# Neighbourhood attention layer on one core: less filler in the first steps, rows split directly, a block of x loaded again earlier

## The chip, the cores and the metric

The kernel runs on one core of one Trainium2 chip. The metric is device time in microseconds (us): 1064.29 us as the median of three runs (1062.66 to 1065.86). The engines are named as in the profile: PE is TensorE (matrix products), PEld its weight loads, DVE is VectorE, ACT is ScalarE, POOL is GpSimd, SP issues nearly all DMAs.

## The reference

One layer of neighbourhood attention over a grid of 32 rows by 64 columns (2048 tokens, 1024 features, 16 heads of 64), in float32:

```python
h = rmsnorm(x, norm_0)
q, k, v, gate = split(h @ w_in, 4)
for each grid row r:                       # rs: first of 8 key rows
    s = q . k * scale                      # 16 query columns against 8 x 32 keys
    s = where(column in window, s + bias, -1e30)
    o = softmax(s) @ v
x = x + (o * silu(gate)) @ w_out
return rmsnorm(x, norm_f)
```

## The kernel before

**Precision.** Every large product is done as three products of float32r parts: an operand is split into h (a copy on ACT) and l = t - h (a subtraction on DVE), and h*h, h*l, l*h are summed in PSUM. So each operand block of 128 x 512 that TensorE uses costs one ACT and one DVE instruction (`split_to`, L441 to L447; the lines of the profile are 443 and 444).

**Stages.** `stage_one` (L501) computes the first half of the tokens: half of the values (`values_of`, L475), and q, k and gate by `seven_products` (L329), in which a 2 x 2 block product is done with seven block products instead of eight, from sums of blocks (T1 to T4 of x, S1 to S4 of the weights). `stage_two` (L727) does the second half: first half of the values of token tiles 8 to 15, in pairs of tiles (`pair`, L753), then twelve units of seven products. Blocks of x are called B11, B12, B21, B22 (first digit: half of the features; second: first or second 512 tokens of the stage). T1 is written over B12's buffers (`t1`, L804), so B12 is lost when the seven products start.

The results q, k, v and the gate go to DRAM. Then come 32 **attention steps**, m = 0 to 31, plus a last one: row groups T = 0 to 3 (8 grid rows each), and in each the 8 head pairs p. A step's order on TensorE is written out in the loop at L1262: filler (`feed`), transposes of the scores of the pair before (`turns`, L948), scores of the next pair (`scores`, L910), values of the pair before (`values`, L968). Between a pair's scores and its transposes, DVE adds the bias and takes the maximum (L931), ACT takes the exponential (L937), DVE the reciprocal (L942), POOL scales (L946). The result o times the gate (L984) is stored to DRAM (`keep`, L986) for the output product.

**Filler.** `feed(n)` (L1219) issues n more products from a list, so that TensorE has work while the scores pass the other engines. The list is first `values_left` (L827): the other half of the values of tiles 8 to 15, 8 tiles of 24 products, 192 in all. Then `outputs` (L1153): 16 row tiles of 128 tokens, 2 column halves, 24 products each. Each step has an amount of products. `amount` (L1207 to L1213) gives the first ten steps `early` = 18.5, moves `first` = 16 from around step 0 to step 1, and spreads the rest of 192 + 546 over the other 22 steps. A clock of products counts (`due`, L279); stores and other late work are queued with a lag in these counts (`store`, L273). An event (a block split, a tile evacuated) lets `feed` borrow up to 6 products (`calm_debt`) for the next 8 counts. If the list has nothing ready, `outputs` yields None and the credit is lost to this step; what isn't done in the steps is done in the tail.

**What filler needs.** `items` (L224) is an ordered list of blocks that are loaded up to 5 ahead (`load_item`) and split (`use_item`) at fixed places (`consume`) or when a product needs them (`need`): 8 blocks of value weights, the 4 blocks of x that T1 has overwritten (loaded again, normalised by L439 and split), 16 blocks of w_out, each set of 8 allowed only after tiles 12 and 16 of the values. In stage two, `also` (L737) consumes six of them.

**Output tiles.** Tile n belongs to row group n // 4. `load_og` (L1026) loads the gated results of all 8 pairs for its 128 tokens once all are stored and 12 counts have passed (`og_ready`, L1018); `split_og` (L1036) splits them. For tiles 12 and 13 (T = 3) only 7 pairs are loaded (`parts`, L1014): the last pair's og is split directly from SBUF when it is made (`direct`, L991). `turns_` (L1131) is the order in which output tiles are used: (0, 0), (1, 0), (2, 0), (0, 1) and so on.

Of the kernel before, what the change touches and what calls it, by code (L numbers as in the profile page):

```python
# [21 lines left out]
NK = D // 128  # L22
# [41 lines left out]
def build(ctx, tc, x, xr, xt, wg, tab, w_out, n0, nf, out):  # L64
# [79 lines left out]
    def load_item(it):  # L144
        kind, a, b = it
        t = raws[it] = raw([128, 512], F32, "raw")
        asked_at[it] = now()
        if kind == "x":
            nc.sync.dma_start(t, xt[a * 128:(a + 1) * 128, b * 512:(b + 1) * 512])
        elif kind == "w":  # L150
            nc.sync.dma_start(t, wg[a[0], :, 512 * b:512 * b + 512])
        else:
            nc.sync.dma_start(t, w_out[a * 128:(a + 1) * 128, b * 512:(b + 1) * 512])

    def use_item(it):
        kind, a, b = it
        state["event"] = clock[0]
        t = raws.pop(it)
        if kind == "x":
            normed("x%d1" % (a // 4 + 1), b, a % 4, t)  # L160
            split_to(hh[a, b], hl[a, b], t, None)
        elif kind == "w":
            t = t.rearrange("p (k c) -> p k c", c=256)
# [563 lines left out]
    def stage_two():  # L727
# [9 lines left out]
        def also(n, i):  # L737
            if then:
                then.pop(0)()
            if n == 0:  # L740
                if i == 0:
                    load_ahead()
                if i in (1, 2, 3, 4):
                    consume(1)
                if i == 5:
                    consume(2)
                if i == 3:
                    for f in (load_tab(0, 0), load_k(0, 0), load_q(0, 0)):
                        f()

        ahead, run = seven_products(units_two, 2, X2, also)
# [52 lines left out]
        def t1(*ks):  # L804
            def g():
# [13 lines left out]
        then = [both(v(0, 10, 11), t1(2, 3)), both(t4(0, 1, 2, 3), form("T4", x21, 0)), form("T4", x21, 1, 2), form("T4", x21, 3)]  # L819
        for k in range(4):  # L820
            hh[k, 2], hl[k, 2] = X2["B11"][k]
            hh[k, 3], hl[k, 3] = X2["B12"][k]
            hh[4 + k, 2], hl[4 + k, 2] = X2["B21"][k]
            hh[4 + k, 3], hl[4 + k, 3] = X2["B22"][k]
        run()

    def values_left():  # L827
        for t in range(8, 16):
# [6 lines left out]
            for k in range(NK):  # L835
                if t == 15 and k in (2, 4) and og_ready(k // 2 - 1):
                    more_og()
                for a in range(2):
                    need(("w", (WV[0] + a, 1), k // 2))
                need(("x", k, c))  # L840
                h, l = wh[k // 2][:, k % 2], wl[k // 2][:, k % 2]
                for m, (x_, w_) in enumerate(((hh[k, c], h), (hh[k, c], l), (hl[k, c], h))):
                    nc.tensor.matmul(p, x_[:, o], w_, start=k == 0 and m == 0, stop=k == NK - 1 and m == 2)  # L843
                    yield 1
# [123 lines left out]
    def values(m):  # L968
# [27 lines left out]

        if T == 3 and p == lastp[T]:
            store(("last", T), 2, direct)
# [15 lines left out]
    def parts(n):  # L1014
        T, i = divmod(n, 4)
        return NK - 1 if T == 3 and i < 2 else NK

# [18 lines left out]
    def split_og(n):  # L1036
# [3 lines left out]
        for j in range(2):  # L1040
            s = slice(4 * j, min(4 * j + 4, parts(n)))
            nc.scalar.activation(h[:, s], t[:, s], AF.Copy)  # L1042
            nc.vector.tensor_tensor(l[:, s], t[:, s], h[:, s].bitcast(F32), OP.subtract)
        G[n] = [(h[:, i], l[:, i]) for i in range(parts(n))]
# [98 lines left out]


    def split_rows():
        n = ready["split"]
        if n < ready["loaded"] and "turn" in ready and place[n] <= ready["turn"] + 3 and now() - late["loaded_at"][n] >= 40 and whole(n) \
                and sum(1 if hasattr(g, "rearrange") else 2 for g in G.values()) <= 6:
            split_og(n)
# [180 lines left out]
```

## Time and profile before

| | |
|---|---|
| time, median of 3 runs | 1064.29 us (1062.66 to 1065.86) |
| the profiled execution's own time | 1064.92 us |
| its span on the core | 1063.1 us |
| PE busy | 1036.2 us, 97% of the span |
| DVE, ACT, POOL busy | 710.6, 483.3, 218.8 us |
| mean granted clock of PE | 0.989 |
| stages one and two | up to about 601 us |
| attention steps | about 601 to 1001 us |
| tail of output products | about 1001 to 1057 us |

The page gives for each engine its busy time and a row of 40 slices of the span, each digit the busy share in tenths; PEclk is the clock that TensorE was granted, in the same slices. "A <- B" in the waits means that an instruction of line A stood idle until B released it: total us, how many times, the longest. Groups have the line, engine, output <- inputs, count, and durations. In a row of windows stand length, then busy time and instruction count of PE, PEld, DVE, ACT and POOL, the granted clock, the DMA share and GB/s.

### The profile page before, as it was taken

What the parts mean: (1) busy time and instruction counts of PE and PEld (TensorE: products, weight loads), DVE (VectorE), ACT (ScalarE), POOL (GpSimd) and SP (SyncE); (2) the same over time, 40 slices, a digit from 0 to 9 for tenths busy, and PEclk for the clock granted to TensorE, in tenths of its full rate; (3) what the DMA queues carried; (4) which work ended last, traced back from release to release, by engine and by line L of the source; (5) the groups of instructions that cost most, each with busy time, mean ns of one, the idle gap of its engine ahead of it and who ended that gap; (6) DMA issues with size and microseconds to landing.
All of it is one profiled execution on the core that took longest, in us unless ns stands there. A gap on an engine that the chain in (4) does not pass through costs nothing.

```text
span 1063.1 us, 19454 instructions
## 1 busy us (share of the span) xinstructions
PE 1036.2 (97%) x7024; PEld 823.3 (77%) x7024; DVE 710.6 (67%) x1595; ACT 483.3 (45%) x1175; POOL 218.8 (21%) x321
## 2 busy tenths in 40 slices
PE   8999999999999999999999999986999999999997
PEld 6888888887887788888888767754777777777786
DVE  5476667768897975556565466565579876876644
ACT  7645323333333443333231356565565665665422
POOL 0000221312311400000000034433333443343100
PEclk9999999999999999999999999988999999999999
DMA  8634444343634433424333877996888988888342
GB/s 303 232 100 114 134 149 137 117 143 126 181 121 128 119 119 95 143 80 137 102 119 85 263 232 257 320 320 215 279 280 286 340 289 271 302 288 272 115 149 79
DMA packets 113192, 200.38 MB, mean 188 GB/s; under 512 B 9992, under 2 KB 44040, under 8 KB 111048
## 3 DMA queue, kind: packets, MB, share of 16 engines
q1 hardware_dynamic: 112664, 198.74, 57.6%
q8 instruction: 55, 0.90, 0.3%
q10 hardware_dynamic: 432, 0.40, 0.1%
q14 instruction: 41, 0.34, 0.1%
HBM read 148.77 MB, written 50.33 MB: 187 GB/s over the span
## 4 chain that ended last, share of the span: by engine, by line
PE 89%; DVE 4%; ACT 2%; DMA 2%; issue 1%; POOL 1%; SPq 1%; POOLq 0%; DVEq 0%; ACTq 0%
PE pp L361 41%; PE pv L485 10%; PE s L923 7%; PE o L980 7%; PE po L1195 6%; PE po L1191 6%; PE po L1193 6%; PE ph L962 4%; PE pv L843 3%; ACT x L937 1%; POOL x L946 1%; DVE l L444 1%; DMA sgd<-sg 1%; ACT h L443 1%; DMA ograw<-ogd 1%
## 5 line engine op out<-in xcount | busy, mean ns | idle before, releaser
L361 PE MATMUL pp<-h,f 128*128 128x512 f32 x768 | 248.5, 389 | 0.0
L946 POOL TENSOR_SCALAR x<-x,st 128x360 f32<-128x360 f32 (+2 forms) x256 | 146.4, 590 | 260.6 <-DVE st L942 228.0
L361 PEld LDWEIGHTS pp<-h,f 128*128 128x128 f32 x768 | 144.2, 188 | 30.5
L361 PE MATMUL pp<-four,f 128*128 128x512 f32 x648 | 161.6, 390 | 0.1
L937 ACT ACTIVATE x<-x,st 128x360 f32<-128x360 f32 (+2 forms) x256 | 139.8, 547 | 28.4 <-DVE st L931 28.4
L361 PE MATMUL pp<-l,f 128*128 128x512 f32 x384 | 149.7, 390 | 0.0
L361 PEld LDWEIGHTS pp<-four,f 128*128 128x128 f32 x648 | 121.5, 188 | 26.4 <-DVE u L374 0.5
L381 POOL TENSOR_TENSOR tmp<-tmp,rb 128x512 f32<-128x512 f32 x36 | 59.2, 1646 | 269.6 <-DVE tmp L379 226.0
L931 DVE CUSTOM_DVE_ANT_0 x<-s,em 128x360 f32<-128x360 f32 (+2 forms) x256 | 108.8, 480 | 7.3 <-PE s L923 6.6
L1191 PE MATMUL po<-woh,gh 128*128 128x512 f32 x252 | 100.4, 398 | 8.3 <-ACT gh L1042 8.3
L1195 PE MATMUL po<-wol,gh 128*128 128x512 f32 x252 | 100.3, 398 | 0.0
L1193 PE MATMUL po<-woh,gl 128*128 128x512 f32 x252 | 99.8, 396 | 0.1
L965 DVE COPY pta<-ph 120x512 f32<-120x512 f32 (+5 forms) x96 | 56.2, 638 | 52.9 <-PE ph L962 52.7
L980 PEld LDWEIGHTS o<-pta,vt 120*64 120x64 f32 (+2 forms) x1024 | 68.5, 137 | 22.8 <-DVE st L931 15.2
L923 PE MATMUL s<-kt,qt 64*64 64x360 f32 (+2 forms) x1024 | 82.1, 442 | 1.9 <-ACT v L318 1.4
L361 PEld LDWEIGHTS pp<-l,f 128*128 128x128 f32 x384 | 72.1, 188 | 15.3
L980 PE MATMUL o<-pta,vt 120*64 120x192 f32 (+5 forms) x1024 | 83.4, 316 | 0.0
L965 ACT ACTIVATE pta<-ph 120x512 f32<-120x512 f32 (+5 forms) x96 | 47.0, 557 | 65.5 <-PE ph L962 65.5
L444 DVE TENSOR_TENSOR f<-raw,f 128x512 fp32r<-128x512 f32 x80 | 55.3, 691 | 29.1 <-ACT f L443 29.1
L369 ACT ACTIVATE p<-pp 128x512 f32<-128x512 f32 x24 | 14.4, 599 | 124.3 <-PE pp L361 124.3
L485 PE MATMUL pv<-wh,h 128*128 128x512 f32 x192 | 63.9, 393 | 2.8 <-ACT h L443 1.2
L379 DVE TENSOR_TENSOR tmp<-pp,u 128x512 f32<-128x512 f32 x48 | 33.1, 690 | 47.9 <-PE pp L361 43.2
(160 smaller groups left out, 1623.8 us busy)
## 6 DMA issues: line engine op xcount, KB each, us to landing
raw<-in_wg_dram SPq DMA_DIRECT2D x124, 256.0 KB, 4.4
em<-in_tab_dram SPq DMA_DIRECT2D x16, 1080.0 KB, 8.9
vd<-v SPq DMA_DIRECT2D x32, 256.0 KB, 5.3
sgd<-sg SPq DMA_DIRECT2D x32, 256.0 KB, 3.7
qt<-qd SPq DMA_DIRECT2D x32, 256.0 KB, 5.3
sgt<-sgd SPq DMA_DIRECT2D x32, 256.0 KB, 8.0
ogd<-og SPq DMA_DIRECT2D x32, 256.0 KB, 2.7
xr<-in_x_dram SPq DMA_DIRECT2D x32, 256.0 KB, 7.9
```

The source lines that it names most:

```text
L361: nc.tensor.matmul(B[n, P], t[:, int(m == 2), c], x[k][int(m == 1)], start=P in (1, 6, 5) and k == 0 and m == 0, stop=k == 3 and m == 2, s ...
L444: nc.vector.tensor_tensor(l, t, h.bitcast(F32), OP.subtract)
L485: nc.tensor.matmul(ps[t], a[:, o], b, start=k == 0 and m == 0, stop=k == NK - 1 and m == 2)
L923: nc.tensor.matmul(pst[s][h * 64:h * 64 + 64], qt[a, C * 128 + h * 64:C * 128 + h * 64 + 64], keys.rearrange("p r (s c) -> p s r c", c=8), ...
L931: nc.vector.tensor_tensor_reduce(X[i, C][s], pst[s], EM[p, T, COL_TYPE[C], s], -1.0, 1e38, OP.add, OP.min, st[:, o:o + 1])
L937: nc.scalar.activation(X[i, C][s], X[i, C][s], AF.Exp, bias=st[:, o:o + 1], scale=-1.0, accum_out=st[:, 4 + o:5 + o])
L946: nc.gpsimd.tensor_scalar(X[i, C][s], X[i, C][s], st[:, o:o + 1], 1.0, op0=OP.mult, op1=OP.mult)
L965: (nc.vector.tensor_copy if h else lambda o, i_: nc.scalar.activation(o, i_, AF.Copy))(to[:k, :, 2 - j, c, h], at[h][:k, :, c])
L980: nc.tensor.matmul(o[s * 64:s * 64 + 64, g0 * 64:g1 * 64 + 64].rearrange("d (g q) -> d g q", q=64), vt[:k, strip, s * 64:s * 64 + 64], t[: ...
L1191: nc.tensor.matmul(p, gh, woh[q, j], start=(i == 0), stop=False)
L1193: nc.tensor.matmul(p, gl, woh[q, j], start=False, stop=False)
L1195: nc.tensor.matmul(p, gh, wol[q, j], start=False, stop=(i == NK - 1))
```

## The change

Four things change.

1. `early` is 16 instead of 18.5 and `first` 14 instead of 16, so the first ten steps get fewer filler products and the later steps more.
2. For T = 0 as for T = 3, the last head pair's result is split directly; tiles 0 and 1 load 7 pairs. They are loaded while tiles 14 and 15 of the values are still being computed, into buffers other than before (`mkp` for tile 0, two halves in `ep` for tile 1), and split at fixed places of tile 15 (`split_first`).
3. The block of x that T1 overwrites is no longer an item of the attention steps. It is loaded again before the last unit of seven products, normalised and split within that unit into buffers of its own, and all 8 blocks of value weights are consumed there too (four, then two and two, instead of six). The first table, keys and queries are loaded at the first product of that unit instead of the fourth.
4. In stage two the pairs of tiles go (8, 9), (10, 11), (12, 13), (14, 15) instead of (8, 9), (12, 13), (14, 15), (10, 11), and the first split of T1 over B12 comes one quarter of a pair later.

```diff
@@ load_item, use_item
-        if kind == "x":
-            nc.sync.dma_start(t, xt[a * 128:(a + 1) * 128, b * 512:(b + 1) * 512])
...
-        if kind == "x":
-            normed("x%d1" % (a // 4 + 1), b, a % 4, t)
-            split_to(hh[a, b], hl[a, b], t, None)
...
-    items += [("x", b, 3) for b in range(4)] + [("o", a, b) for b in range(2) for a in range(NK)]
+    items += [("o", a, b) for b in range(2) for a in range(NK)]
@@ stage_two: also
+            if (n, i) == (-1, 5):
+                again = mkp([128, 3, 512], F32, "again")
+                L2["x12"] = [again[:, k] for k in range(3)] + [lp([128, 512], F32, "again")]
+                for k in range(4):
+                    load_x(2, "x12", k, L2["x12"][k])
             if n == 0:
                 if i == 0:
                     load_ahead()
-                if i in (1, 2, 3, 4):
-                    consume(1)
-                if i == 5:
-                    consume(2)
-                if i == 3:
                     for f in (load_tab(0, 0), load_k(0, 0), load_q(0, 0)):
                         f()
+                    for k in range(4):
+                        normed("x12", 3, k, L2["x12"][k])
+                if i in (1, 2, 3):
+                    consume(1)
+                if i == 4:
+                    consume(1)
+                    X2["B12"] = [(xs([128, 512], F32R, "h"), xs([128, 512], F32R, "l")) for _ in range(4)]
+                if i in (4, 5):
+                    for k in (0, 1) if i == 4 else (2, 3):
+                        split_to(*X2["B12"][k], L2["x12"][k], None)
+                if i in (5, 6):
+                    consume(2)
@@ stage_two: pairs
-        pair(0, (12, 13), both(v(0, 8, 9), block("B22", x22, 2, 3)), both(t123(0), t123(3)), t123(1), t123(2))
-        pair(0, (14, 15), v(0, 12, 13), form("T3", x22, 0, 1), both(form("T3", x22, 2, 3), lambda: ahead(-9, -1)),
+        pair(0, (10, 11), both(v(0, 8, 9), block("B22", x22, 2, 3)), both(t123(0), t123(3)), t123(1), t123(2))
+        pair(0, (12, 13), v(0, 10, 11), form("T3", x22, 0, 1), both(form("T3", x22, 2, 3), lambda: ahead(-9, -1)),
...
-        pair(0, (10, 11), both(v(0, 14, 15), form("T2", x11, 2, 3), lambda: ahead(-8, -1)), both(lambda: ahead(-7, -1), t1(0, 1)),
-             both(lambda: ahead(-6, -1), lambda: ahead(-5)), both(lambda: ahead(-4), lambda: ahead(-3), lambda: ahead(-2)))
+        pair(0, (14, 15), both(v(0, 12, 13), form("T2", x11, 2, 3), lambda: ahead(-8, -1)), lambda: ahead(-7, -1),
+             both(lambda: ahead(-6, -1), lambda: ahead(-5), t1(0, 1)), both(lambda: ahead(-4), lambda: ahead(-3), lambda: ahead(-2)))
@@ values_left
-                if t == 15 and k in (2, 4) and og_ready(k // 2 - 1):
+                if t >= 14 and ready["loaded"] < 2 and og_ready(ready["loaded"]):
                     more_og()
+                if t == 15 and k in (4, 7):
+                    split_first(k // 7)
...
-                need(("x", k, c))
@@ values
-        if T == 3 and p == lastp[T]:
+        if T in (0, 3) and p == lastp[T]:
             store(("last", T), 2, direct)
@@ parts
-        return NK - 1 if T == 3 and i < 2 else NK
+        return NK - 1 if T in (0, 3) and i < 2 else NK
@@ load_og
-        G[n] = t = wp([128, NK, 128], F32, "ograw")
+        if n == 1:
+            G[n] = [ep([128, 4, 128], F32, "ograw") for _ in range(2)]
+            for j, t in enumerate(G[n]):
+                w = min(4 * j + 4, parts(n)) - 4 * j
+                nc.sync.dma_start(t[:, :w], ogd[T][:, i, 4 * j:4 * j + w])
+            return
+        t = (wp if n else mkp)([128, NK, 128], F32, "ograw")
+        G[n] = [t[:, :4], t[:, 4:]]
@@ new
+    def split_first(n):
+        if ready["split"] == n < ready["loaded"] and whole(n):
+            split_og(n)
+            ready["split"] += 1
@@ amounts
-    early, end_of_it = 18.5, 24
+    early, end_of_it = 16, 24
     amount = [early] * 10
-    first = 16
+    first = 14
```

More of the change, by code (lines that the diff above doesn't have):

```diff
@@ L147, in load_item @@
         asked_at[it] = now()
-        if kind == "x":
-            nc.sync.dma_start(t, xt[a * 128:(a + 1) * 128, b * 512:(b + 1) * 512])
-        elif kind == "w":
+        if kind == "w":
             nc.sync.dma_start(t, wg[a[0], :, 512 * b:512 * b + 512])
@@ L158, in use_item @@
         t = raws.pop(it)
-        if kind == "x":
-            normed("x%d1" % (a // 4 + 1), b, a % 4, t)
-            split_to(hh[a, b], hl[a, b], t, None)
-        elif kind == "w":
+        if kind == "w":
             t = t.rearrange("p (k c) -> p k c", c=256)
@@ L1147, in split_rows @@
         if n < ready["loaded"] and "turn" in ready and place[n] <= ready["turn"] + 3 and now() - late["loaded_at"][n] >= 40 and whole(n) \
-                and sum(1 if hasattr(g, "rearrange") else 2 for g in G.values()) <= 6:
+                and sum(1 if len(g) == 2 else 2 for g in G.values()) <= 6:
             split_og(n)
```

15 lines of the change are left out of this document (7 added, 8 removed).

## The prediction, made before the change was run

> **What bounds the kernel now.** I read the page first, then busy time by stage, then the waits of TensorE, and last the chain of work through the stage where waits stand.
>
> ```profile
> PE 1036.2 (97%) x7024; PEld 823.3 (77%) x7024; DVE 710.6 (67%) x1595; ACT 483.3 (45%) x1175; POOL 218.8 (21%) x321
> PE   8999999999999999999999999986999999999997
> PEclk9999999999999999999999999988999999999999
> ```
>
> TensorE is busy for 1036.2 of 1063.1 us, so 26.9 us of idle time is all that better ordering alone can win, plus whatever a lowered clock adds to the busy part. The change takes no matmul away: 192 value products and 768 output products are fed into the attention steps before and after, and what isn't fed there is done in the tail. So the question is where the 26.9 us lie. The slices show one dip, two thirds along, with the clock down beside it. By stage (columns: length, then busy time of PE, PEld, DVE, ACT, POOL, then the clock, DMA share, GB/s):
>
> ```profile
> 600.00:640.00 40.00, 36.84 (x333) 26.66 (x332) 23.33 (x75) 20.11 (x61) 9.49 (x20) 0.96 0.81 244
> 640.00:711.00 71.00, 66.35 (x784) 50.86 (x782) 44.10 (x147) 45.17 (x137) 32.02 (x59) 0.98 0.88 288
> 711.00:755.00 44.00, 35.60 (x360) 25.31 (x357) 27.29 (x78) 24.89 (x69) 14.97 (x24) 0.84 0.72 253
> 755.00:1000.00 245.00, 245.00 (x2700) 186.33 (x2701) 185.02 (x581) 145.73 (x441) 90.50 (x169) 1.00 0.83 278
> 1000.00:1063.10 63.10, 56.67 (x259) 46.40 (x255) 29.27 (x78) 15.03 (x37) 0.00 (x0) 0.97 0.36 120
> ```
>
> From 755 to 1000 us TensorE has no idle time: filler put there costs exactly its own length. Between 600 and 755 us 3.2 + 4.7 + 8.4 = 16.3 us are idle, and the last 6.4 us belong to the final tile, which the change doesn't touch. What the idle time waits for:
>
> ```profile
> PE po L1191 <- ACT gh L1042: 8.3, 1, 8.3
> PE ph L962 <- POOL x L946: 3.8, 4, 1.8
> PE pv L843 <- ACT wh L443: 1.5, 1, 1.5
> PE pv L843 <- DVE wl L444: 0.3, 1, 0.3
> PE s L923 <- ACT v L318: 1.4, 1, 1.4
> PE pv L485 <- ACT h L443: 1.2, 3, 0.4
> PE ph L962 <- POOL x L946: 0.3, 1, 0.3
> ```
>
> The first two are one event. The value products run out at step 9 (698 to 711 us): the transposes of that step stand behind nothing, so they wait for POOL's normalised scores (3.8 us in four waits). The output products that should follow need the first row tile, and it can be loaded only once the last head pair of its row group is stored and twelve counts have passed; at step 10 TensorE waits 8.3 us for its first split. The next three rows are the start of attention: the last weight block (L443, L444) is split only when the filler asks for it, behind the exponentials, and the evacuation of a value tile (L318) stands behind four blocks of x that are being normalised and split again. The last 1.2 us are in stage two. The 0.3 is step 5, below.
>
> The waits also lower the clock. These are the three stretches at half clock, and two other windows of the same length:
>
> ```profile
> 609.15:612.57 3.42, 3.42 (x12) 2.17 (x14) 0.00 (x0) 0.60 (x1) 0.00 (x0) 0.50 0.99 389
> 708.14:714.97 6.83, 5.08 (x55) 3.40 (x59) 4.75 (x9) 2.37 (x5) 2.38 (x2) 0.50 1.00 336
> 721.80:732.03 10.23, 4.85 (x11) 3.55 (x12) 3.10 (x5) 2.71 (x5) 0.71 (x2) 0.50 0.98 343
> 605.74:609.15 3.41, 1.62 (x7) 0.81 (x6) 1.32 (x4) 2.15 (x8) 0.00 (x0) 1.00 1.10 165
> 622.80:626.21 3.41, 2.06 (x25) 0.97 (x26) 2.71 (x6) 2.45 (x5) 0.00 (x0) 1.00 0.58 177
> ```
>
> TensorE worked 3.42 + 5.08 + 4.85 = 13.35 us at half clock; at full clock that is 6.7 us. The window before the first drop held 1.62 us of work, and the window that held 2.06 us was followed by none: a drop here seems to need a 3.41 us window that is more than about half idle. The Trainium skill, TensorE: Matmul & The Clock Gate, "What's actually happening", asks for an idle window of about 3.4 us before the clock falls. By that wording only the drop after the 8.3 us wait hangs on a wait removed here, which would make the clock's term 2.4 instead of 6.7 us and the time 1048.0. The trace disagrees: its first drop followed a window with 1.62 us of work in it.
>
> **The change, part by part.** *Fewer early filler products.* Per step the order is filler, transposes, scores, values:
>
> ```profile
> 688.73 1.36 PE ph L962 x44
> 690.09 2.18 PE s L923 x29
> 692.27 2.54 PE o L980 x32
> 694.81 3.65 PE pv L843 x15
> 629.60 4.53 PE pv L843 x19
> 640.21 5.67 PE pv L843 x24
> 651.96 4.54 PE pv L843 x19
> ```
>
> One product is 3.65 / 15 = 0.24 us. I followed feed's arithmetic: a step takes its amount in whole products, and within eight counts of an event it borrows up to six. For the amounts of before this gives 19, 24, 19, 16, 15, 22, 15, 1 for steps 2 to 9; the rows show 19, 24, 19 for steps 2 to 4 and 15 for step 8. Value products end at count 192, one into step 9. With 16 and 14 it gives 23, 33, 14, 15, 22, 16, 12, 17, 13, 22, 20 for steps 0 to 10, and count 192 falls five products into step 10. The 2.5 products a step that are taken away come back as 22.95 to 24.23 in the later steps, where TensorE has no idle time to lose: cost nothing, gain nothing. The gain is in steps 9 and 10, which get work.
>
> What covers less now are the steps up to 8. From a step's scores to its next transposes TensorE has 2.18 + 2.54 + 0.24 per product; the scores must meanwhile pass DVE, ACT and POOL:
>
> ```profile
> 658.09 0.67 PE s L923 x8
> 661.88 5.76 POOL L946 TENSOR_SCALAR x<-x,st 128x264 f32<-128x264 f32 x8 [4.95 <-DVE st L942]
> 693.97 3.87 POOL L946 TENSOR_SCALAR x<-x,st 128x264 f32<-128x264 f32 x8 [7.37 <-DVE st L942]
> ```
>
> That takes 693.97 + 3.87 - 690.09 = 7.75 us alone, and 661.88 + 5.76 - 658.09 = 9.55 us while DVE splits four blocks of the output weight. Step 5 of before was the second kind, with 16 products: 4.72 + 16 x 0.243 = 8.61, and it waited 0.3, so 0.64 us of the lag is free (the transposes need the last score late). With 12 products, the fewest, TensorE's side is 4.72 + 2.92 + 0.64 = 8.28 us: over 7.75, so a plain step waits for nothing even then. Splits of the output weight fall on step 4 (three, beside 22 products), step 5 (four, beside 16: the same 0.3 again) and step 6 (one, beside 12: 7.75 plus a quarter of 1.9 is 8.2, just covered). Bounds: 0, and 9.55 - 8.28 = 1.3 us in each of seven steps, 9 us. I take 0.5, near the plain rows.
>
> *Second load of the block of x moved.* Four loads of 256 KB, four normalisations and four splits go from attention step 0 and 1 into the end of stage two, and the two weight blocks left over go there too.
>
> ```profile
> 582.00:604.00 22.00, 22.00 (x104) 17.86 (x106) 11.53 (x18) 6.91 (x12) 0.21 (x2) 1.00 0.79 244
> L439 DVE SCALAR_TENSOR_TENSOR raw<-raw,g,rb x4: 745/769/974, 615.8 to 622.2; 128x512 f32<-128x512 f32 x4
> L443 ACT ACTIVATE h<-raw x4: 630/632/633, 616.6 to 623.0; 128x512 fp32r<-128x512 f32 x4
> L444 DVE TENSOR_TENSOR l<-raw,h x4: 691/692/693, 617.3 to 623.6; 128x512 fp32r<-128x512 f32 x4
> land<-in_xt_dram SPq DMA_DIRECT2D x21, 256.0 KB, 5.0
> 595.65 0.69 DVE L379 TENSOR_TENSOR tmp<-pp,u 128x512 f32<-128x512 f32 x1 [0.83 <-PE pp L361]
> 604.26 0.43 DVE L931 CUSTOM_DVE_ANT_0 x<-s,em 128x264 f32<-128x264 f32 x1 [1.03 <-PE s L923]
> ```
>
> In the last unit DVE gets 4 x 0.77 + 6 x 0.69 = 7.2 us and ACT 6 x 0.63 = 3.8 us (the weight blocks have the shape of the x splits). DVE then has 18.7 of 22 us to do and ACT 10.7: it fits, but not evenly. After its fifth product, whose evacuation starts at 595.65 us, DVE has, by my count, about 10 us of work in order, evacuations, gate products and splits, before the first scores' maxima, which started at 604.26 us; they start about a microsecond later. Behind DVE's new work queue the unit's evacuations, which no product of the unit waits for, and the maxima, behind which some 30 filler products (7 us) stand before the first transposes. The loads are issued one product before the unit starts and take 5.0 us; the normalisations are queued some 5 us after that, so a late landing would block DVE for a microsecond or two, with nothing urgent behind it. On SP's queue the four loads come before the weight loads, and the first table, keys and queries are issued three products earlier. What goes: 1.5 + 0.3 + 1.4 = 3.2 us of waits and the first stretch at half clock. Bounds of the new cost: 0, and the 3.2 us back; I take 0.5.
>
> *Order of pairs in stage two.* Pair (12, 13) came second and waited for the splits of its own block (the 1.2 us). Now (10, 11) is second, which needs blocks already split, and (12, 13) follows 48 products later. The overwrite of the block by T1 moves one quarter later, behind its readers. Gain 1.2 us, bounded below by 0.
>
> *Direct split of the first row group's last pair.* Tiles 0 and 1 now need seven stored pairs, not eight. The seventh is written in step 8 at count 156, twelve counts later (168) tile 0 is loaded, tile 1 at 171; the splits follow at 180 and 189 and the products at 192. The load is not behind step 9's store on SP's queue, and has about a whole step before ACT reaches the split. ACT and DVE get one split of 256 columns more, under 1 us in a step with room. So the 8.3 and 3.8 us go, and with them the clock's two later stretches.
>
> *Further on.* The output products of a row group now end about 11 counts sooner relative to the next group's tiles: at counts 384 and 576 a tile is split just when it is wanted, where before it was split eight or more products earlier. One such split cost 8.3 us when its load was late; here the load is issued a step earlier. Bounds 0 and 2 x 8.3; I take 0.5 each, 1.0 in all, since the 245 us without a wait already hold such hand-overs.
>
> **The sum**, against the profiled execution's own 1064.92 us (span 1063.1; the median of three runs is 0.6 lower): removed 8.3 + 3.8 + 3.2 + 1.2 = 16.5 and the clock's 6.7, together 23.2; charged 0.5 + 0.5 + 1.0 = 2.0. That is 1064.9 - 21.2 = 1043.7 us.
>
> **Rivals.** *Waits in the early steps that drop the clock*, the one that ends slower. If the steps of the first row group lose their cover, each waits up to 1.3 us, and each such wait may cost a window of 3.41 us at half clock, 1.7 us more. Eight steps times 3.0 is 24 us, which with the 1.5 of the other charges gives 1064.9 - 23.2 + 24 + 1.5 = 1067.2. It decides from waits of some 1.4 to 1.8 us in a window, the idle part of the two windows above. For it: 12 and 13 products are fewer than any step had in this stretch. Against it: the plain lag of 7.75 us is covered even by 12, and the 0.3 us wait left the clock alone. The same page of the Trainium skill, Part 4, says that transposes don't count as busy in the same way; by that a step's 1.36 us of transposes would add to its wait and 0.3 us might be enough; no step here shows it. All eight: chance 0.04. *In a few steps only*, two or three drops or a late load of x: 5 to 8 us given back, 1049 to 1052, chance 0.10.
>
> *The rows are still not ready at count 192*, so that the change doesn't do what it says: the load waits on SP's queue, or the split on ACT stands behind its landing. Then 8.3, 3.8 and the later clock stretches (5.0) stay, 3.2 + 1.2 + 1.7 is won: about 1059 us, chance 0.08. Against it: by the counts the load is issued 24 products and a whole step's attention work (6 us) before its use. *The same, and the start of attention waits as before* (DVE's backlog in place of the late weight split): 1062 to 1064, chance 0.03. *The first two drops hang on something else than the waits*: 3.42 + 5.08 us stay at half clock, 4.3 us come back, 1048.0, chance 0.04; against it, each stands right behind a wait. (This is the wording of the skill's page, above.) A further 0.01 goes to slower by other ways.
>
> **How the numbers follow.** The forecast has the other 0.70, with 1040.5 to 1048 as its own range: below, all charges at nothing (1041.7) and a microsecond for the spread of runs; above, the start's 3.2 and another microsecond or two. With the drops that stay and the few steps the range is 1040.5 to 1052, holding 0.84. About 0.3%, 3.2 us, is what a measurement of this kernel can tell from no change; faster by more than that is the forecast, the drops that stay, the few steps and the rows that aren't ready, 0.92; within it 0.03; slower 0.05.
>
> **What would show it.** TensorE's slices have no dip near two thirds; idle between 600 and 755 us falls from 16.3 to under 3 us; the clock stays at 1.00 through attention; "po <- ACT gh" of 8.3 is gone from the waits; steps 2 to 8 show 14, 15, 22, 16, 12, 17, 13 filler products; the tail's output products shrink by about 27 (by feed's arithmetic 744 products are fed by the end of the steps, against 717). Stages one and two up to 600 us last 1.2 us less. I would be wrong if "ph <- POOL" appears in most of the early steps, if a half-clock stretch follows them, or if TensorE waits on a DMA of tile 0.

## The result, and the profile after

The changed kernel takes 1049.53 us (median of four runs, 1049.04 to 1053.99), against 1064.32 us for the kernel before: ratio 0.9871, 95% interval 0.984 to 0.9901. (The ratio goes by means, and the one run of 1053.99 lifts it; by medians it is 0.9861.) Its profiled execution took 1049.58 us with a span of 1047.8 us, 15.3 us under the profiled execution of before. The forecast was 1043.7, its range 1040.5 to 1052. So the direction and the place were right, and 5.9 us of the forecast gain of 21.2 us are missing.

The page's first lines, and by stage the same columns as before:

```profile
PE 1033.4 (99%) x7024; PEld 819.7 (78%) x7024; DVE 706.6 (67%) x1596; ACT 482.2 (46%) x1176; POOL 214.4 (20%) x321
PE   9999999999999999999999999999999999999997
PEclk9999999999999999999999999999999999999999
```

```profile
600.00:640.00 40.00, 40.00 (x439) 30.42 (x438) 22.46 (x88) 22.98 (x77) 12.75 (x31) 1.00 0.90 272
640.00:711.00 71.00, 68.03 (x788) 51.79 (x789) 45.59 (x150) 46.66 (x139) 29.97 (x56) 1.00 0.93 307
711.00:755.00 44.00, 44.00 (x497) 32.70 (x492) 33.10 (x98) 30.95 (x90) 17.55 (x28) 1.00 0.89 312
755.00:985.00 230.00, 226.62 (x2393) 168.15 (x2392) 168.30 (x537) 130.90 (x398) 81.75 (x155) 1.00 0.80 267
```

The dip is gone and the clock stays at 1.00 until the last tile. Between 600 and 755 us 3.0 us are idle, where it was 16.3. But the stretch from 755 us on, which had no idle time at all, now has 3.4 us of it. And TensorE's busy time fell by only 2.9 us, although three stretches at half clock, worth 6.7 us by the prediction's count, are gone: something else that counts as busy grew. The waits of TensorE from 600 us on say where to look:

```profile
PE ph L968 <- POOL x L952: 1.6, 2, 1.2
PE po L1212 <- DVE gl L1057: 1.4, 2, 1.1
PE s L929 <- DMA kt<-kd: 1.2, 1, 1.2
PE po L1210 <- ACT gh L1056: 1.0, 1, 1.0
PE s L929 <- DVE pta L971: 0.9, 2, 0.5
```

Line numbers are those of the changed kernel: L968 are the transposes, L929 the scores, L1056 and L1057 the splits of output tiles, L971 the copies of the transposes out of PSUM. Of the waits that the prediction lists, only the 0.3 us of step 5 is left, inside the first row; the rest of that row and the other rows are new. The chain of work that ended last shows the filler of steps 2, 3, 4, 7, 8 and 9, product for product as feed's arithmetic had it; the tail has 216 products instead of 243, the 27 fewer that were forecast:

```profile
619.99 3.44 PE pv L849 x14
629.51 3.63 PE pv L849 x15
639.31 5.25 PE pv L849 x22
...
672.06 4.08 PE pv L849 x17
682.22 3.21 PE pv L849 x13
691.91 5.21 PE pv L849 x22
```

The rest comes from TensorE's timeline, step by step, as the time from the first transpose, score or filler product to the first of the next kind. These are the first transposes of steps 9 and 10, before and after:

```profile
705.29 0.27 PE L962 MATMUL ph<-ident,x 64*120 64x64 f32 x1
733.22 1.50 PE L962 MATMUL ph<-ident,x 64*120 64x64 f32 x44
```

```profile
697.05 1.50 PE L968 MATMUL ph<-ident,x 64*120 64x64 f32 x44
708.52 0.44 PE L968 MATMUL ph<-ident,x 64*120 64x64 f32 x5
```

Three gains and four losses make up the difference:

- The transition. From the transposes of step 9 to those of step 10, 27.9 us with 15 products of step 10 between them (705.29 to 733.22 us) became 11.5 us with 20 (697.05 to 708.52). With the five products more, at 0.23 us, that is 17.6 us won.
- The start of attention, from the first scores to the first transposes, with these transposes and the scores behind them: 17.8 + 2.8 + 2.9 us became 13.0 + 1.4 + 2.2 us, with four products fewer: 6.0 us won.
- Up to the first scores 2.4 us are won: the three waits of stage two (1.2), 0.7 by a first block that landed sooner at the kernel's start and is no part of the change, and 0.5 in small pieces.
- Lost: the scores of steps 10 to 31 last 4.4 us longer, 60.1 us instead of 55.7. In steps 15, 16, 17, 19, 21, 24 and 26 they take 0.5 to 1.2 us over their usual 2.58 or 2.26; before, three steps took 0.4 to 0.5 more (16, 18 and 23, 1.3 us together). Most of this counts as busy, which is where the clock's gain went.
- Lost: the filler of steps 18 and 26, in which tiles 4 and 8 begin, is 1.7 and 1.4 us too long for its products.
- Lost: the transposes of step 10 wait 1.2 us for POOL and take 1.9 us more.
- Lost: in step 6 the scores wait for their keys, 1.3 us more than that step's delay before.

Won 26.0, lost 10.8: 15.2 against the measured 15.3 us.

### The profile page after: what moved, and what is told of

It reads as the page before. It is cut to its first block, busy times and chain, and to the rows that moved or that the text cites. A ratio compares the mean times of both kernels' runs of the same rounds, so it can differ in the third digit from the quotient of the medians.

```text
span 1047.8 us, 19452 instructions
## 1 busy us (share of the span) xinstructions
PE 1033.4 (99%) x7024; PEld 819.7 (78%) x7024; DVE 706.6 (67%) x1596; ACT 482.2 (46%) x1176; POOL 214.4 (20%) x321
## 4 chain that ended last, share of the span: by engine, by line
PE 86%; DVE 6%; DMA 3%; ACT 2%; issue 2%; SPq 1%; POOL 0%; DVEq 0%; POOLq 0%; ACTq 0%
PE pp L356 41%; PE pv L480 8%; PE s L929 7%; PE o L986 7%; PE po L1210 5%; PE po L1214 5%; PE po L1212 5%; PE ph L968 4%; PE pv L849 4%; DMA ograw<-ogd 1%; DVE l L439 1%; DMA kt<-kd 1%; ACT x L943 1%; DMA qt<-qd 1%; DVE land L434 1%
## 5 line engine op out<-in xcount | busy, mean ns | idle before, releaser
L952 POOL TENSOR_SCALAR x<-x,st 128x360 f32<-128x360 f32 (+2 forms) x256 | 142.0, 573 | 257.8 <-DVE st L948 243.9
L1212 PE MATMUL po<-woh,gl 128*128 128x512 f32 x248 | 97.6, 393 | 1.4 <-DVE gl L1057 1.4
L1214 PE MATMUL po<-wol,gh 128*128 128x512 f32 x248 | 97.5, 393 | 0.0
L971 DVE COPY pta<-ph 120x512 f32<-120x512 f32 (+5 forms) x96 | 56.0, 637 | 51.8 <-PE ph L968 51.8
L986 PEld LDWEIGHTS o<-pta,vt 120*64 120x64 f32 (+2 forms) x1024 | 68.5, 137 | 22.8 <-DVE st L937 15.2
L929 PE MATMUL s<-kt,qt 64*64 64x360 f32 (+2 forms) x1024 | 83.8, 439 | 2.2 <-DMA kt<-kd 1.2
L971 ACT ACTIVATE pta<-ph 120x512 f32<-120x512 f32 (+5 forms) x96 | 47.0, 557 | 81.7 <-PE ph L968 81.7
L438 ACT ACTIVATE f<-raw 128x512 fp32r<-128x512 f32 x80 | 49.3, 625 | 33.1 <-PE pp L356 12.5
```

The source lines that it names most:

```text
L929: nc.tensor.matmul(pst[s][h * 64:h * 64 + 64], qt[a, C * 128 + h * 64:C * 128 + h * 64 + 64], keys.rearrange("p r (s c) -> p s r c", c=8), ...
L952: nc.gpsimd.tensor_scalar(X[i, C][s], X[i, C][s], st[:, o:o + 1], 1.0, op0=OP.mult, op1=OP.mult)
L971: (nc.vector.tensor_copy if h else lambda o, i_: nc.scalar.activation(o, i_, AF.Copy))(to[:k, :, 2 - j, c, h], at[h][:k, :, c])
L986: nc.tensor.matmul(o[s * 64:s * 64 + 64, g0 * 64:g1 * 64 + 64].rearrange("d (g q) -> d g q", q=64), vt[:k, strip, s * 64:s * 64 + 64], t[: ...
L1212: nc.tensor.matmul(p, gl, woh[q, j], start=False, stop=False)
L1214: nc.tensor.matmul(p, gh, wol[q, j], start=False, stop=(i == NK - 1))
```

## The experiments

Theory A is the forecast's: the gain lies in the transition, which needs the later end of the value products and the direct split together, and in the start of attention. B and C are that one of the two does it alone. The other letters are for what came back. The experiments ran in three later batches, in which the kernel before took 1064.19, 1063.84 and 1064.33 us; the changed kernel's 1049.53 us, against which most of them are held, rests on its four runs above. A difference of a microsecond or two between medians is therefore told apart only where the runs don't overlap.

**The amounts of before in the changed kernel.**

```diff
-    early, end_of_it = 16, 24
+    early, end_of_it = 18.5, 24
...
-    first = 14
+    first = 16
```

> The changed kernel with the amounts of before (18.5 and 16). Theory A (the forecast's: the transition needs fewer early products and the direct split together): value products end at count 191 in step 8 again, the first row tile is asked for at count 192 before the last pair's direct split exists, 8.5 counts of step 9 are lost, its transposes wait for POOL and its first split waits: 1053 to 1057 us. Theory B (the direct split alone closes the gap, the amounts do nothing): within 1.5 us of the changed kernel's 1049.5.

Measured: 1064.15 us, ratio to the kernel before 1.0001 (0.9992 to 1.0009). Everything but two numbers of the change is there, and the whole gain is gone. Neither theory had that. The waits on the split of output tiles in its trace, in step 9 and in step 17, and the two windows at the latter:

```profile
PE po L1210 <- ACT gh L1056: 4.1, 1, 4.1
```

```profile
PE po L1210 <- ACT gh L1056: 10.4, 1, 10.4
```

```profile
804.34:807.75 3.41, 0.00 (x0) 0.00 (x0) 0.00 (x0) 0.00 (x0) 0.00 (x0) 1.00 1.00 313
807.75:817.99 10.24, 4.45 (x23) 2.97 (x25) 1.29 (x2) 1.76 (x4) 0.00 (x0) 0.50 0.85 331
```

The first is the transition, within what A said. The second is a hole of the same kind one row group later. The kernel before had lost some 27 counts of credit in steps 9 and 10 (717 products fed by the end of the steps, against 744), and so its output products came late enough that row group 1 was stored before they reached it: 368 products were done by the end of step 17. With the direct split and the old amounts little is lost, 391 products are done by then, and tile 4 is asked for and wanted at the same count, 384. TensorE waits 10.4 us, and a stretch of 10.24 us at half clock follows. With 16 and 14 it is 375, and the tile's load is issued nine products ahead, at 797.2 us. So the smaller amounts do a second job that the prediction didn't see: closing the first hole lets the output products run 23 ahead, and the amounts hold them back by 16 of these.

**The amounts alone, in the kernel before.**

```diff
-    early, end_of_it = 18.5, 24
+    early, end_of_it = 16, 24
...
-    first = 16
+    first = 14
```

> The kernel before with only the amounts of the change (16 and 14). By feed's arithmetic step 9 gets 16 products and count 192 falls 11 products into step 10, where tile 0 is loaded and wanted at once. Theory A: the 3.8 us of step 9 go, a wait of 4 to 7 us for tile 0's load stays, with a clock stretch behind it, and the start of attention keeps its 3.2 us: 1056 to 1060 us. Theory C (the amounts alone carry the gain): 1052 to 1054.

Measured: 1065.57 us, ratio 1.0013 (1.0005 to 1.0022): no gain, a little slower. C is out; A was 6 us too hopeful. The wait for tile 0 is there, and its stretch at half clock lasts as long as the longest of before:

```profile
PE po L1191 <- ACT gh L1042: 8.1, 2, 7.0
```

```profile
714.49:724.73 10.24, 5.76 (x13) 4.27 (x14) 3.10 (x5) 2.71 (x5) 0.00 (x0) 0.50 1.01 380
```

The filler of step 10 takes 16.2 us for 26 products that need 6.1. The transition's 17.6 us thus become 7.7, and the losses of the later steps, which come with these amounts, take them all: the scores of steps 10 to 31 last 60.8 us, 5.1 more than before, and the filler of steps 18 and 26 is 1.9 and 1.5 us too long, as in the changed kernel.

**The direct split of row group 0 left out of the changed kernel.**

```diff
-        if T in (0, 3) and p == lastp[T]:
+        if T == 3 and p == lastp[T]:
...
-        return NK - 1 if T in (0, 3) and i < 2 else NK
+        return NK - 1 if T == 3 and i < 2 else NK
```

> The changed kernel without the direct split of row group 0: tiles 0 and 1 load eight pairs. By the arithmetic they are loaded at counts 183 and 186 and wanted at 192, all in step 10. Theory A: TensorE waits 3 to 6 us for the load in step 10 and a half-clock stretch may follow: 1053 to 1058 us. Theory C (the amounts alone suffice): within 1.5 us of 1049.5.

Measured: 1054.49 us (1051.11 to 1056.39), ratio 0.9909 (0.9894 to 0.9923): 5.0 us more than the changed kernel, as A had it. In the profiled run, the fastest of the six, TensorE waits 2.3 us in step 10, and no half-clock stretch follows there:

```profile
PE po L1210 <- ACT gh L1056: 2.1, 1, 2.1
PE po L1212 <- DVE gl L1057: 0.2, 1, 0.2
```

That run is only 1.5 us behind the changed kernel's. Four of the others took 1054.2 to 1056.4 us, and three of them had a granted clock of 0.996 against its 0.999; what they lost no trace shows. So by the medians the direct split is worth 5 us beside the new amounts, of which the trace accounts for a part.

**The block of x in the attention steps again.** The old `also`, the items of kind x and six weight blocks in stage two, everything else as changed.

```diff
+    items += [("x", b, 3) for b in range(4)] + [("o", a, b) for b in range(2) for a in range(NK)]
...
+                need(("x", k, c))
```

> The changed kernel with the block of x loaded, normalised and split in the attention steps as before, and six weight blocks in stage two. Theory A (forecast: 3.2 us of waits at the start of attention and a clock stretch of 1.7 us belong to this part): 1053 to 1055.5 us, the waits on wh L443 and on the evacuation are back. Rival: the start's waits come from the amounts of step 0 and not from this part: within 1 us of 1049.5.

Measured: 1056.71 us, ratio 0.9929 (0.9916 to 0.9941), 7.2 us more, above A's range. The waits are the ones of before (1.2, 0.9 and 0.3 us instead of 1.5, 1.4 and 0.3), so they belong to this part:

```profile
PE pv L843 <- ACT wh L443: 1.2, 1, 1.2
PE s L923 <- ACT v L318: 0.9, 1, 0.9
PE pv L843 <- DVE wl L444: 0.3, 1, 0.3
```

The clock explains why it is more than the start alone. The first stretch is the start's. The second follows step 10, where the transposes wait 1.2 us for POOL; the changed kernel has the same wait, but there the clock stayed up:

```profile
607.25:610.66 3.41, 3.41 (x21) 1.49 (x20) 1.38 (x8) 0.90 (x3) 0.29 (x1) 0.50 0.96 371
713.07:716.48 3.41, 2.08 (x45) 1.67 (x44) 1.50 (x3) 0.67 (x2) 2.32 (x4) 1.00 0.97 259
716.48:719.89 3.41, 3.41 (x28) 1.54 (x29) 2.49 (x7) 1.91 (x5) 0.00 (x0) 0.50 1.07 410
```

**The order of pairs in stage two as before**, everything else as changed (the four `pair` lines and `then` of before).

> The changed kernel with stage two's pairs of tiles in the order of before. Forecast's step: the three waits of 0.4 us on ACT's splits in pair (12, 13) are back, 1.0 to 1.5 us more, 1050.5 to 1051. Rival: the splits that follow run late by the same amount in either order, and the time stays within 0.5 us of 1049.5.

Measured: 1052.15 us (1051.49 to 1053.09), ratio 0.9885 (0.9872 to 0.9899), 2.6 us more by the medians. The changed kernel's slowest run took longer than all of these, so the size is uncertain. The three waits of 0.4 us are back in its trace, which is the forecast's 1.2 us:

```profile
PE pv L480 <- ACT h L438: 1.2, 3, 0.4
```

In the two profiled runs the whole difference, 2.0 us, is there before the first scores (602.87 us against 600.87); what makes up the 0.8 us beside the three waits is open.

**The scaling of a finished tile three counts later.**

```diff
-            store(("y", n), 9, scale)
+            store(("y", n), 12, scale)
```

> The changed kernel with one number changed: the scaling of a finished output tile on DVE (1.4 us for two halves) is queued 12 counts after its root instead of 9. In the changed kernel it falls on the last count of a step of 24 and stands on DVE just ahead of the copies of the transposes, so the next scores wait for banks (3.1 to 3.7 us instead of 2.6 in the steps where a tile ends); with 23 counts it fell into the next step. Theory D (this lock of phases gave back about 4 us): scores return to 2.6 us and the time is 1045 to 1047.5. Rival E (the long scores come from other work, and the scale does as much harm in its new place): within 1 us of 1049.5.

Measured: 1045.14 us (1044.04 to 1045.8), ratio 0.9827 (0.9812 to 0.9841): 4.4 us faster than the changed kernel, and D holds. In step 15 DVE's timeline of the changed kernel has the scaling just ahead of the copies that free the PSUM banks, and the scores are long:

```profile
771.77 1.42 DVE L1121 SCALAR_TENSOR_TENSOR y<-y,st,acc 128x512 f32<-128x512 f32 x2
773.10 1.75 DVE L971 COPY pta<-ph 120x512 f32<-120x512 f32 x3
```

```profile
773.16 3.18 PE L929 MATMUL s<-kt,qt 64*64 64x360 f32 x32
```

With the scaling later the copies come first, at 772.53, the scaling at 779.07, and the scores take their usual time:

```profile
772.53 1.75 DVE L971 COPY pta<-ph 120x512 f32<-120x512 f32 x3 [0.73 <-PE ph L968]
...
779.07 1.72 DVE L1121 SCALAR_TENSOR_TENSOR y<-y,st,acc 128x512 f32<-128x512 f32 x2
```

```profile
773.23 2.65 PE L929 MATMUL s<-kt,qt 64*64 64x360 f32 x32
```

The scores of steps 10 to 31 last 54.1 us in its trace, 6.0 less than in the changed kernel and 1.6 less than before, so the lag of 12 also removes long scores that the kernel before had; the filler of step 18 gives 0.7 back.

The arithmetic behind it: the root (the reciprocal root of the norm, which the scaling multiplies by) is computed after the second part of a step's feed, 10 + 0.34 x 14.2 = 14.8 counts in; 9 more is 23.8, still inside a step of 24. But this isn't the difference to the kernel before, though the expectation had it so. There the scaling also stands just ahead of the copies, in steps 17, 19, 21, 25 and 27, but it ends before the copies could start, and costs nothing. Step 17, whose first transpose is at 818.04 us:

```profile
816.95 1.41 DVE L1107 SCALAR_TENSOR_TENSOR y<-y,st,acc 128x512 f32<-128x512 f32 x2
818.77 1.75 DVE L965 COPY pta<-ph 120x512 f32<-120x512 f32 x3 [0.42 <-PE ph L962]
```

What differs is when the scaling runs. In that step the root starts 4.3 us ahead of the transposes, and the sum that takes a finished output half out of PSUM (L1075) comes behind it. In the changed kernel's steps 15 to 17 that sum (L1089) comes first, 3.3 us ahead of the transposes, the root follows at 2.6, and the scaling ends 1.5 us into them. The run with the amounts alone has the same 1.5 us, and the same scores of 3.1 us, in these steps, so it is the amounts that bring it. That the sum's place is the reason is read from the traces; no run moved it alone.

**Row tiles loadable after 6 counts instead of 12.**

```diff
-        return all(("og", p, T) in written and clock[0] - stored_at[p, T] >= 12 for p in range(NP)
+        return all(("og", p, T) in written and clock[0] - stored_at[p, T] >= 6 for p in range(NP)
```

> The changed kernel with one number changed: a row tile counts as loadable 6 counts after its last pair's store instead of 12. Theory F (the forecast's hand-over at counts 384 and 576: the load lands after the tile is wanted): tiles 4 and 8 are issued six products, 1.4 us, sooner, the waits on gh and gl (1.0 and 1.4 us) shrink or go, 1047 to 1048.5. Rival G: the split itself is queued behind other work on ACT and DVE, so an earlier load changes nothing: 1049 to 1050.

Measured: 1048.71 us, ratio 0.9861 (0.9846 to 0.9876): 0.8 us by the medians, between F's range and G's, and not told apart from the changed kernel. The waits show that both are half right: the wait on gh is gone, and in its place stands a second one of 1.15 us on gl:

```profile
PE po L1212 <- DVE gl L1057: 2.3, 2, 1.1
```

**And tiles 4 and 8 split at the start of their step.** The load as in the run before, and:

```diff
         begin(m)
+        if m in (18, 26):
+            split_first(ready["split"])
         feed(10)
```

> The changed kernel with row tiles loadable after 6 counts, and tiles 4 and 8 split at the start of steps 18 and 26 instead of when they are wanted. With the load alone sooner the wait on gh went and waits of 1.15 us on gl stayed at both places: the split is made only when wanted. Theory J (the split's own time, ACT then DVE, is that wait): both waits go, 2.3 us and what lies around them, 1046 to 1047.5. Rival K (ACT and DVE are held up by the split before step 18's own work, and the transposes then wait): 1048.5 to 1050.

Measured: 1047.54 us (1046.93 to 1048.33), ratio 0.9842 (0.9828 to 0.9855). At the edge of J's range, 2.0 us under the changed kernel, and all four runs are faster than its fastest. Both waits are gone from the trace. Part of the gain is given back, as K said, in the next transposes: those of step 18 take 2.0 us instead of 1.4.

**The final norm's weights loaded later.**

```diff
-            if t == 13:
+            if t == 14:
                 late_loads()
```

> The changed kernel with the two loads of the final norm's weights, and the first residual load, issued at value tile 14 instead of 13. In the changed kernel they stand on SP's queue in step 5 beside four loads of the output weight, and the keys for step 6 are issued 2 to 3 us late; TensorE waits 1.2 us for them. Theory H: that wait goes, 1048 to 1049. Rival I: the DMA engines themselves are full there, the wait stays: 1049.5 within 0.5.

Measured: 1052.89 us, ratio 0.9899 (0.9885 to 0.9914): 3.4 us slower by the medians, against both theories (one of the changed kernel's runs was slower still, the other three faster than all of these). There is no wait on the keys in step 6; there is one in step 8 instead, longer, and the clock falls behind it:

```profile
PE s L929 <- DMA kt<-kd: 2.1, 1, 2.1
```

```profile
684.18:687.59 3.41, 1.52 (x45) 1.28 (x44) 1.75 (x3) 1.46 (x3) 0.00 (x0) 1.00 1.07 322
687.59:691.00 3.41, 3.16 (x24) 1.59 (x28) 1.32 (x5) 0.97 (x3) 0.00 (x0) 0.50 1.06 281
```

So these loads do make keys late, as H had it, and in the short steps there is no free place for them further on. That their old place was the cause of the wait in step 6 isn't shown: the runs without the direct split and with the old pairs issue these loads where the changed kernel does, and their traces have no wait on the keys either.

**Both repairs together, and the loads earlier.** First the scaling at 12 with the sooner split:

> The kernel of g1_split_sooner with the scaling 12 counts after its root. If the two losses are independent: the 4.4 us of the scaling (1049.5 to 1045.1) and what g1 gains add up, 1042 to 1043.5. If the shifted scaling meets the earlier splits on DVE: 1044 to 1046.

Measured: 1042.43 us (1041.51 to 1045.86), ratio 0.9791 (0.9778 to 0.9804). The two gains add up, as the first expectation had it, and this is the fastest version: 7.1 us under the changed kernel, 21.9 under the one before. K's price is there too: in its trace the transposes of step 18 take 3.3 us instead of 1.4. Then, besides, the final norm's weights at value tile 10:

> The kernel of g2_scale_and_split with the loads of the final norm's weights and the first residual issued at value tile 10 (step 1 or 2) instead of 13 (step 5); at tile 14 they only moved the late keys from step 6 to step 8, where the wait was longer and the clock dropped. Theory H (SP's queue and the DMA engines of those steps are what is short, and steps 1 and 2 have room): the wait of 1.2 us on the keys goes and none comes, 1 to 1.5 us under g2. Rival: the wait only moves again, to the keys of step 2 or 3, same as g2 or up to 2 us more.

Measured: 1043.36 us, ratio 0.9801 (0.9788 to 0.9814), not told apart from the run without it. No wait is put down to the keys in either trace; the run without the earlier loads has one of 0.9 us at the same place, put down to the copies of the transposes. So whether the earlier loads are worth anything stays open.

**12 as the early amount.**

```diff
-    early, end_of_it = 16, 24
+    early, end_of_it = 12, 24
```

> The changed kernel with 12 instead of 16 as the early amount: by the arithmetic 13, 12, 12, 12, 17, 12, 7, 12 products in steps 2 to 9. Theory A (7.75 us of lag is covered by 12 products, 9.55 beside splits by 17): small waits, about 1 us in steps 6 and 8 (7 products: 4.72 + 1.7 + 0.64 = 7.1 against 7.75), no half clock: 1050 to 1052. Rival (the forecast's slower case: waits of the early steps lower the clock): several half-clock stretches between 610 and 700 us, 1056 or more.

Measured: 1056.65 us (1054.37 to 1059.34), ratio 0.9938 (0.9921 to 0.9955), 7.1 us slower than with 16. The size is the rival's, two half-clock stretches included, but the waits are not on POOL:

```profile
PE s L929 <- DMA kt<-kd: 7.7, 3, 3.3
PE ph L968 <- POOL x L952: 2.2, 3, 1.3
```

```profile
682.82:689.65 6.83, 5.18 (x34) 2.15 (x36) 3.13 (x14) 2.99 (x11) 0.01 (x1) 0.50 0.67 206
699.88:706.71 6.83, 5.86 (x40) 2.78 (x42) 3.82 (x16) 3.67 (x13) 0.69 (x2) 0.50 1.02 334
```

POOL's lag cost 2.2 us, near A's 2. What the short steps lack is the time for their loads: keys take 7.9 to 9.5 us to land in the changed kernel's steps 4 to 6, and a step with 12 products lasts some 9 us (631.2 to 640.3 us in this run).

## Why the prediction came out right, point by point

The measured 1049.53 us lies in the range 1040.5 to 1052, but not in the forecast's own, 1040.5 to 1048. The part of the range where it lies, 1049 to 1052, was there for another case, with a chance of 0.10: two or three drops of the clock, or a late load of x, in the first steps. Neither is in the trace. So the place of the gain was right for the reasons given, and that the loss of 5.9 us stayed inside the range is in part luck. By its parts, against what the sum charged: 4.4 in the scores, 2.2 in the hand-overs, 2.7 in steps 6 and 10; against that 1.6 more won at the start of attention, 1.2 before it and 0.5 in the transition, 6.0 in all.

- **The transition.** Forecast 8.3 + 3.8 us of waits and 5.0 us of clock, 17.1; the trace gives 17.6. Right. What the step left out is that it rests on the amounts twice over. "The gain is in steps 9 and 10, which get work" is true only because the output products are also held back for the next hand-over; the first experiment shows the same hole at count 384 otherwise.
- **The start of attention.** Forecast 3.2 + 1.7 with 0.5 charged, 4.4; measured 6.0 in the trace and 7.2 by undoing the part, of which one stretch at half clock in step 10 is an effect of phase. The mechanism was right, the size too small.
- **Stage two.** Forecast 1.2; the waits went as said, and undoing it brings them back. What it costs in time, 2.6 by the medians, is uncertain by more than a microsecond. The other 1.2 us won before the first scores aren't the prediction's: 0.7 of it is a load at the kernel's start.
- **The early steps.** Charged 0.5. The plain steps wait for nothing, as worked out, and step 5 waits 0.34 us as before. The 1.3 us lost there are keys that land late in step 6 of this trace (not of every run), which the prediction didn't look at: it took SP's queue for the moved loads only, and not for what four loads of the output weight and two of the norm's weights, issued just ahead of these keys, can do to them once the steps are shorter. Step 10 was taken as covered and lost 1.9. The split of tile 1 holds up the reciprocal there until 706.7 us, and beside three splits of the output weight POOL then takes 3.67 us for four instructions; the four before them took 2.19.
- **The hand-overs at 384 and 576.** Named, with bounds of 0 and 16.6 and 1.0 taken; they cost 3.2. The reason for the 1.0, that the later steps "already hold such hand-overs", was weak: before, the load of tile 4 was issued 24 products ahead and its split was done eight ahead; now the load is issued nine ahead, 9.8 us before the split.
- **The step that failed** is "the 2.5 products a step that are taken away come back ... in the later steps, where TensorE has no idle time to lose: cost nothing, gain nothing". They cost 4.4 us in the scores: with the new amounts DVE's scaling runs about a microsecond and more later against the transposes and holds up the copies behind it. One number that moves the scaling away gives 4.4 us of the time back (it also removes 1.6 us of long scores that the kernel before had), and the amounts alone bring the same long scores into the kernel before.
- **The rivals.** The early waits that drop the clock are real (12 as early amount), from a lower amount on than the change has, and through the keys and not mainly through POOL. That the rows wouldn't be ready at 192 didn't happen, thanks to the direct split: without it TensorE waits 2.3 us for them.
- **The clock.** The row-based rule, that a window of 3.41 us more than about half idle is followed by half clock, held in before for its two windows; later runs blur it between 1.8 and 2.1 us of work (below). The wording of a whole idle window, the Trainium skill's, did not hold. All three drops went with their waits, as the sum had it; that two of them would stay, by that wording, is refuted for this kernel.

## What to carry to other kernels

A queue of filler that ran dry at one place had been delayed by it at every later place, so closing one hole has to be followed through the next hand-overs, count by count, before it is called a gain. Filler that is moved to a stage without waits isn't free either: it shifts when another engine's work falls just ahead of the next step's critical copies, and one lag in the schedule was worth 4.4 us here. In short steps look at the time a load takes to land beside the step's own length, not only at the engines' busy time.

## What the runs showed of the hardware

Half clock doesn't need a long wait. The same 1.2 us wait on POOL in step 10 left the clock alone in the changed kernel and brought a stretch of 3.41 us at half clock in the run with x in the steps. The drops and returns of a run lie whole multiples of 3.41 us apart (in before 609.15, 612.57, 708.14, 714.97, 721.80, 732.03), so the windows run on a grid of their own, and it matters whether a wait falls into one window or is cut by an edge. From 609.15 to 732.03 us are 36 windows, so one lasts 122.88 / 36 = 3.4133 us. In the changed kernel the last drop begins at 1044.41 us; 98 windows earlier lies an edge at 709.90 us, and it cuts that wait:

```profile
706.49:709.90 3.41, 2.47 (x15) 1.71 (x13) 2.52 (x5) 1.51 (x3) 2.88 (x3) 1.00 0.97 242
709.90:713.32 3.42, 3.03 (x59) 2.25 (x63) 2.21 (x4) 1.49 (x3) 0.79 (x2) 1.00 0.97 333
```

In the run with x in the steps, the window that was followed by a drop had 2.08 us of work, all of it but one instruction transposes; the window of before with 2.06 us, all scores, was followed by none. That would agree with the Trainium skill, TensorE: Matmul & The Clock Gate, Part 4, which says that transposes don't count as busy in the same way. But a window of the run with 12 as the early amount has 2.11 us of work, 44 of its 49 instructions transposes, and no drop behind it, and one of the run with the later scaling has 1.78 us of output products and none either, less than the 1.85 us of value products (603.84 to 607.25 us) that the first half-clock stretch of the run with x in the steps followed:

```profile
669.16:672.57 3.41, 2.11 (x49) 1.70 (x52) 2.30 (x4) 1.42 (x4) 2.04 (x3) 1.00 0.85 205
803.40:806.81 3.41, 1.78 (x9) 1.13 (x7) 2.53 (x5) 1.29 (x5) 1.31 (x2) 1.00 1.02 382
```

So between about 1.8 and 2.1 us neither the busy time of a window nor its share of transposes decides by itself here whether the clock falls; what does is open. (The ends of matrix products in a profile are modelled, and these edges are counted back from a later drop.)
